# A transformer backbone on one core: the later modulation weights and the position-bias broadcasts go from SyncE's DMA queue to GpSimd's

## The chip, the cores and the metric

The kernel runs on one NeuronCore of a Trainium2 chip. The metric is the device time of one execution in microseconds (us). Engines are named as in the profile: PE (TensorE, matmuls), DVE (VectorE), ACT (ScalarE), POOL (GpSimd) and SP (SyncE, which here only issues DMAs). Each engine executes its instructions in the order of its own program.

## The reference

Two layers over 2048 latent tokens and 256 context tokens, of width 1024, in float32. Cut to what matters here:

```python
def _modulation(cvec, w_mod, b_mod):            # w_mod: (2 layers, 1024, 3072)
    return jnp.split(jax.nn.silu(cvec) @ w_mod + b_mod, 3, axis=-1)   # shift, scale, gate
```

Each layer normalises its tokens, scales and shifts them by the modulation (one vector for the latent tokens, from c, and one for the context tokens, from c_ctx), projects them to q, k, v and gate columns, runs two attention mixers, and adds the gated output projection to the residual. In layer 0 one of the mixers ("B") is a two-dimensional neighbourhood attention with a learned bias table b_rpb by relative position, 8 heads of 15 x 31 entries.

## The kernel before, in words

Work is cut into 9 pairs of token tiles (256 tokens each, the ninth being ctx). A tile scheduler sets the order of the instructions on every engine from a model of their times; the program's text gives the dependencies and a few constraints, so a changed line can move instructions on engines that the line does not name.

The first 330 us of layer 0, by `layer_front` (L939 and on), go like this.

- **Modulation, `mod_cols` (L144).** The 3072 columns of each layer are cut into 12 groups of 256; `j` counts them. Each group loads a 1 MB tile `wmod` (L148), from a pool of 4 buffers. For the first 8 groups of layer 0 (shift and scale, needed at once) and three groups of layer 1, PE multiplies `wmod` directly. For the other 13 groups DVE does the product: for the latent and, mostly, the context vector, 8 instructions on 128 x 256 elements accumulate into `macc` (the first on L159, seven on L161), 22 such sums or 176 instructions in all; then PE adds over partitions (pO<-macc), DVE copies the row (`m`, L171), PE transposes it and DVE adds the bias (`mod`, L177). The four remaining groups of layer 0 and the 12 of layer 1 form the filler `mods`, stepped in the program's text inside the loop over pairs of the second and third chunk (L1006 to L1008), behind the load of ctx (`xload[8]`) on the loading engine's queue and behind `shlast` on DVE's. `mod_scales` (L180) turns the first 8 groups into scales and shifts; its norm `hrs` is a POOL instruction.
- **hT, `hT_make` (L251).** For each pair, x is loaded, scaled by DVE (`xt`, L248), transposed by PE, scaled and shifted (`hf`, on DVE L272 and on ACT L270), cast to float16 (on DVE L274 and on ACT L276), and POOL subtracts to get the low half (L277), four times for a pair, 36 in all.
- **Projections, `project` (L306).** In chunks of 256 columns: qb0, kb0, vb0, and so on; 48 matmuls `pmm<-wk,hT` for a pair. qb0 runs beside the making of hT. q and k results are split into high and low halves `HL` (ACT L361, DVE L367), transposed by a DMA on SP's queue (L333) into `qkst` and stored (L335). v results go through `vst` (ACT L415, DVE L417).
- **Bias table, `rel_tables` (L598).** b_rpb and a reversed copy are each loaded into a tile `rp` of 120 x 128; then each of its rows is written 64 times into a DRAM scratch table `rpad`, by 4 DMAs for each table (L609), each of 1920 rows of 512 bytes. The B heads read them back in a skewed form (`braw`, L584), from 290 us on. In the text they stand at the third pair of the third chunk, held behind `self.wload`, the last weight load, on the loading engine's queue (L1003).

All these DMAs are issued by SP, in its order.

Of the kernel before, what the change touches and what calls it, by code (L numbers as in the profile page):

```python
# [16 lines left out]
P = 128  # L17
# [18 lines left out]
class Build:  # L36
# [107 lines left out]
    def mod_cols(self, l, j, wp, on_pe):  # L144

        nc = self.nc
        wt = wp.tile([P, 8, 256], F32, name="wmod")
        self.wlast = nc.sync.dma_start(out=wt, in_=self.I["w_mod"][l, :, j * 256:(j + 1) * 256].rearrange("(k p) j -> p k j", p=P))  # L148
        na = 1 if l == 1 and j >= 8 else 2
        terms = []  # L150
        if on_pe:
            terms = [(self.cT[:, :, k], wt[:, k]) for k in range(8)]
        else:
            for a in range(na):
                o = wp.tile([P, 256], F32, name="macc", bufs=4)
                for k in range(8):
                    c = self.cT[:, a, k:k + 1]
                    if k == 0:
                        nc.vector.tensor_scalar(out=o, in0=wt[:, k], scalar1=c, scalar2=None, op0=ALU.mult)  # L159
                    else:  # L160
                        nc.vector.scalar_tensor_tensor(out=o, in0=wt[:, k], scalar=c, in1=o, op0=ALU.mult, op1=ALU.add)  # L161
                    if k == 3:
                        yield
                yield
                terms.append((self.sel[:, 2 * a:2 * a + 2], o))
        pool = (self.pmm, "pmm") if l == 0 and j < 8 else (self.pO, "pO")
        ps = pool[0].tile([P, 512], F32, name=pool[1])
        for i, (l_, r_) in enumerate(terms):
            self.mm(ps[0:2, 0:256], l_, r_, i == 0, i == len(terms) - 1)
        m2 = wp.tile([2, 256], F32, name="m2", bufs=2)  # L170
        nc.vector.tensor_copy(out=m2, in_=ps[0:2, 0:256])  # L171
        pool = (self.ptr, "ptr") if l == 0 and j < 8 else (self.pO, "pO")
        ps2 = pool[0].tile([P, 512], F32, name=pool[1])
        for g in range(2):
            nc.tensor.transpose(out=ps2[:, 2 * g:2 * g + 2], in_=m2[:, g * P:(g + 1) * P], identity=self.idf[:2, :2])
        bias = self.bT[:, 24 * l + 2 * j:24 * l + 2 * j + 2].unsqueeze(2).broadcast_to([P, 2, 2])
        nc.vector.tensor_tensor(out=self.mod[l][:, 2 * j:2 * j + 2, :], in0=ps2[:, 0:4].rearrange("p (g a) -> p g a", a=2),  # L177
                                in1=bias, op=ALU.add)
# [419 lines left out]
    def rel_tables(self, pool):  # L598


        nc = self.nc
        self.rpad = []
        for t, name in enumerate(("b_rpb", "b_rpb_r")):
            rp = pool.tile([120, P], F32, name=f"rp{t}")
            nc.vector.memset(rp, 0.0)
            nc.sync.dma_start(out=rp[:, 48:79], in_=self.I[name].rearrange("o h r c -> (o h r) c"))
            rpad = self.dp.tile([120, 64, P], F32, name=f"rpad{t}")
            for i in range(0, 120, 30):
                nc.sync.dma_start(out=rpad[i:i + 30], in_=rp[i:i + 30].unsqueeze(1).broadcast_to([30, 64, P]))  # L609
            self.rpad.append(rpad)  # L610

    def b_tables(self):
# [969 lines left out]
```

## Time and profile before

| | |
|---|---|
| median of 3 runs | 3745.75 us (3744.8 to 3751.46) |
| the profiled execution | 3762.25 us |
| its span, first to last instruction | 3760.4 us |
| mean granted clock of PE | 0.983 |
| busy: PE, DVE, ACT, POOL | 3565.1, 2603.6, 2403.2, 2347.4 us |

The span is the profile's own time; 1.85 us of the profiled execution lie around it. Busy time is the time in which an engine executes, without the issuing of DMAs. The granted clock is the share of TensorE's full clock that the chip allowed.

### The profile page before, as it was taken

What the parts mean: (1) busy time and instruction counts of PE and PEld (TensorE: products, weight loads), DVE (VectorE), ACT (ScalarE), POOL (GpSimd) and SP (SyncE); (2) the same over time, 40 slices, a digit from 0 to 9 for tenths busy, and PEclk for the clock granted to TensorE, in tenths of its full rate; (3) what the DMA queues carried; (4) which work ended last, traced back from release to release, by engine and by line L of the source; (5) the groups of instructions that cost most, each with busy time, mean ns of one, the idle gap of its engine ahead of it and who ended that gap; (6) DMA issues with size and microseconds to landing.
All of it is one profiled execution on the core that took longest, in us unless ns stands there. A gap on an engine that the chain in (4) does not pass through costs nothing. (4 is left out here: it accounts for less than half of the span.)

```text
span 3760.4 us, 103033 instructions
## 1 busy us (share of the span) xinstructions
PE 3565.1 (95%) x42242; PEld 2946.7 (78%) x42242; DVE 2603.6 (69%) x6585; ACT 2403.2 (64%) x4094; POOL 2347.4 (62%) x1822
## 2 busy tenths in 40 slices
PE   7869998989999999999999999999989999999998
PEld 5648987878976777677767888999878888887775
DVE  5746779798567676666666888777565656656666
ACT  5215655556668887787864556666567777776665
POOL 3203456676358888788864454435358878877775
PEclk9989999999999999999999999999999999999999
DMA  7884634343261111111135444412351211211222
GB/s 235 214 210 103 124 88 101 80 92 101 67 213 40 44 60 38 48 49 49 33 114 135 104 101 100 105 58 78 113 168 30 78 47 56 62 37 51 101 98 103
DMA packets 455488, 350.64 MB, mean 93 GB/s; under 512 B 207782, under 2 KB 407270, under 8 KB 454502
## 3 DMA queue, kind: packets, MB, share of 16 engines
q1 hardware_dynamic: 455014, 344.06, 33.1%
q8 instruction: 330, 5.41, 0.6%
q14 instruction: 144, 1.18, 0.1%
HBM read 207.43 MB, written 106.90 MB: 84 GB/s over the span
## 5 line engine op out<-in xcount | busy, mean ns | idle before, releaser
L783 POOL TENSOR_TENSOR L<-Pm,H 128x1024 f16<-128x1024 f32 (+1 forms) x640 | 1240.1, 1958 | 293.0 <-ACT H L781 213.1
L82 PE MATMUL pmm<-wk,hT 128*128 128x256 f16 x10848 | 1365.5, 276 | 45.4 <-DVE HL L367 19.3
L82 PEld LDWEIGHTS <-hT 128*128 128x128 f16 x10848 | 1034.9, 99 | 189.6 <-issue 35.9
L752 DVE TENSOR_REDUCE mx<-pM 128x1 f32<-128x512 f32 (+1 forms) x1280 | 787.1, 634 | 514.0 <-PE pM L82 503.8
L82 PE MATMUL pO<-V,H 128*128 128x65 f16 (+3 forms) x9216 | 785.0, 207 | 3.2 <-DVE ya L1260 1.4
L82 PEld LDWEIGHTS <-H 128*128 128x128 f16 x9216 | 644.7, 98 | 100.5 <-DVE o L1454 3.6
L82 PE MATMUL pO<-V,L 128*128 128x65 f16 (+1 forms) x4608 | 710.8, 209 | 8.0 <-POOL L L783 7.4
L514 POOL TENSOR_TENSOR Pl<-Sb,Ph 128x640 f16<-128x640 f32 (+4 forms) x288 | 439.0, 1524 | 427.5 <-ACT Ph L513 248.3
L781 ACT CAST H<-Pm 128x1024 f16<-128x1024 f32 (+1 forms) x640 | 602.9, 959 | 11.8 <-PE pO L82 1.9
L82 PE MATMUL pS<-Qt,KH 128*128 128x256 f16 x2304 | 559.1, 273 | 2.6 <-DMA KH<-qk 1.4
L82 PE MATMUL pS<-Q,KL 65*128 65x256 f16 x2304 | 550.0, 274 | 0.0
L82 PEld LDWEIGHTS <-L 128*128 128x128 f16 x4608 | 442.9, 98 | 53.1 <-POOL L L783 14.9
L82 PE MATMUL pM<-KH,Qt 128*128 128x512 f16 (+1 forms) x1280 | 448.3, 359 | 16.4 <-DVE mx L752 10.3
L778 ACT ACTIVATE Pm<-pS,esc_c 128x1024 f32<-128x1024 f32 (+1 forms) x320 | 323.3, 1026 | 207.9 <-PE pS L82 181.7
L82 PEld LDWEIGHTS <-KL 65*128 65x128 f16 x3824 | 374.4, 98 | 83.3 <-issue 28.2
L778 ACT ACTIVATE Pm<-pS,esc_a 128x1024 f32<-128x1024 f32 (+1 forms) x320 | 324.6, 1027 | 156.1 <-PE pS L82 104.0
L82 PE MATMUL pX<-wo,yT 128*128 128x512 f16 x1488 | 390.2, 380 | 1.5 <-ACT yT L890 1.3
L82 PEld LDWEIGHTS <-KH 128*128 128x128 f16 x2304 | 227.3, 99 | 59.2 <-issue 7.0
L82 PEld LDWEIGHTS <-yT 128*128 128x128 f16 x1632 | 154.2, 98 | 134.4 <-ACT yT L890 6.2
L513 ACT CAST Ph<-Sb 128x640 f16<-128x640 f32 (+4 forms) x288 | 219.4, 762 | 51.1 <-PE pO L82 41.0
L82 PE MATMUL pT<-Q,K 128*128 128x128 f16 x1520 | 216.5, 220 | 18.1 <-ACT Sb L509 6.4
L82 PE MATMUL pT<-Q,KL 65*128 65x128 f16 x1520 | 214.5, 220 | 4.4 <-DVE Q L490 4.4
(295 smaller groups left out, 5536.5 us busy)
## 6 DMA issues: line engine op xcount, KB each, us to landing
qk<-qkst SPq DMA_DIRECT2D x104, 256.0 KB, 2.4
wmod<-w_mod SPq DMA_DIRECT2D x24, 1024.0 KB, 8.4
xo<-x SPq DMA_DIRECT2D x48, 512.0 KB, 3.5
xt<-x SPq DMA_DIRECT2D x34, 512.0 KB, 4.9
G<-zz SPq DMA_DIRECT2D x68, 256.0 KB, 2.5
x<-xo SPq DMA_DIRECT2D x34, 512.0 KB, 2.9
wst<-w_in_even SPq DMA_DIRECT2D x13, 1024.0 KB, 5.8
wst<-w_in_odd SPq DMA_DIRECT2D x13, 1024.0 KB, 5.5
```

Of the source, the lines that this page charges most:

```text
L82: return self.nc.tensor.matmul(out=out, lhsT=l, rhs=r, start=s, stop=e, skip_group_check=skip)
L513: nc.scalar.copy(out=H[:, :n * P], in_=Sb[:, :n * P])
L514: nc.gpsimd.tensor_tensor(out=L[:, :n * P], in0=Sb[:, :n * P], in1=H[:, :n * P], op=ALU.subtract)
L752: nc.vector.tensor_reduce(out=mx[:, j:j + 1], in_=ps[:, :n], op=ALU.max, axis=AX.X)
L778: nc.scalar.activation(out=Pm[:, :n], in_=S[:, :n], func=AF.Exp, scale=esc[0], bias=LNP)
L781: nc.scalar.copy(out=H[:, :n], in_=Pm[:, :n])
L783: eng.tensor_tensor(out=L[:, :n], in0=Pm[:, :n], in1=H[:, :n], op=ALU.subtract)
```

## The change

DMAs of wmod are issued by SP only for the first 8 groups of layer 0; the other 16 are issued by POOL. The 8 broadcasts into rpad are issued by POOL as well. What is computed does not change.

```diff
-        self.wlast = nc.sync.dma_start(out=wt, in_=self.I["w_mod"][l, :, j * 256:(j + 1) * 256].rearrange("(k p) j -> p k j", p=P))
+        q = nc.sync if l == 0 and j < 8 else nc.gpsimd
+        self.wlast = q.dma_start(out=wt, in_=self.I["w_mod"][l, :, j * 256:(j + 1) * 256].rearrange("(k p) j -> p k j", p=P))
...
             for i in range(0, 120, 30):
-                nc.sync.dma_start(out=rpad[i:i + 30], in_=rp[i:i + 30].unsqueeze(1).broadcast_to([30, 64, P]))
+                nc.gpsimd.dma_start(out=rpad[i:i + 30], in_=rp[i:i + 30].unsqueeze(1).broadcast_to([30, 64, P]))
```

The changed file has one line more from L149 on, so its L160 and L162 are L159 and L161 of before, and so on.

The order on SP, at the place of the rpad broadcasts, before:

```order
L606 DMA rp_2467<-b_rpb_r 120x31
L148 DMA wmod<-w_mod 128x8x256
L609 DMA rpad_2462<-rp_2459 1920x1x128 x2
L335 DMA qk_90<-qkst 128x4x256
L333 DMA_TRANSPOSE qkst<-HL 128x4x128 x2
L609 DMA rpad_2462<-rp_2459 1920x1x128 x2
L148 DMA wmod<-w_mod 128x8x256
L609 DMA rpad_2470<-rp_2467 1920x1x128 x4
L333 DMA_TRANSPOSE qkst<-HL 128x4x128
L335 DMA qk_90<-qkst 128x4x256
```

The same place on SP, now:

```order
L607 DMA rp_2467<-b_rpb_r 120x31
L336 DMA qk_90<-qkst 128x4x256
L334 DMA_TRANSPOSE qkst<-HL 128x4x128 x2
L336 DMA qk_90<-qkst 128x4x256
L334 DMA_TRANSPOSE qkst<-HL 128x4x128 x4
L336 DMA qk_90<-qkst 128x4x256 x2
```

Between the transposes and stores of q and k on SP there is no broadcast and no wmod load any more.

On POOL, the first rows behind the start of the program, now; before there was no DMA among them (`hT_449` and `hT_504` are the first two pairs, `xrs` and `wrs` norms of x and of a weight chunk):

```order
L121 TENSOR_TENSOR wrs<-n_309,mhalf 128x1
L149 DMA wmod<-w_mod 128x8x256 x4
L121 TENSOR_TENSOR xrs<-xr,mhalf 128x2
L121 TENSOR_TENSOR hrs<-n_428,mhalf 128x1
L278 TENSOR_TENSOR hT_449<-hf_455,hT_449 128x2x256
...
L278 TENSOR_TENSOR hT_504<-hf_510,hT_504 128x2x256
L149 DMA wmod<-w_mod 128x8x256
L278 TENSOR_TENSOR hT_504<-hf_529,hT_504 128x2x256
L149 DMA wmod<-w_mod 128x8x256
...
L149 DMA wmod<-w_mod 128x8x256
L121 TENSOR_TENSOR wrs<-n_1582,mhalf 128x1
L610 DMA rpad_2462<-rp_2459 1920x1x128 x4
L610 DMA rpad_2470<-rp_2467 1920x1x128 x4
L149 DMA wmod<-w_mod 128x8x256
L121 TENSOR_TENSOR wrs<-n_2384,mhalf 128x1
```

Of the 16 wmod loads 14 now stand ahead of the last hT subtraction, the fifteenth behind it, and the last behind the eight rpad broadcasts.

On DVE, where the first macc stand. Before they come beside the last two pairs (`hf_1219`, `hf_1315`; 20 of the 176 stand ahead of the last cast of hT):

```order
L272 TENSOR_SCALAR hf_1219<-pS,sc_82,sh_84 128x256 x2
L248 TENSOR_SCALAR xt<-xt,xrs 128x1024 x2
L159 TENSOR_SCALAR macc<-wmod,cT 128x256 x2
L161 SCALAR_TENSOR_TENSOR macc<-wmod,cT,macc 128x256 x3
L272 TENSOR_SCALAR hf_1238<-pT,sc_82,sh_84 128x256 x2
```

Now they begin ahead of the first pair (`hf_455`) and go on between all of them:

```order
L197 TENSOR_SCALAR sh_84<-mod_80,hrs 128x8x2
L160 TENSOR_SCALAR macc<-wmod,cT 128x256 x2
L442 TENSOR_SCALAR esc_b_3014<-F_0qb_305,hn_86 128x1
L273 TENSOR_SCALAR hf_455<-pS,sc_82,sh_84 128x256 x2
L162 SCALAR_TENSOR_TENSOR macc<-wmod,cT,macc 128x256 x5
L273 TENSOR_SCALAR hf_474<-pT,sc_82,sh_84 128x256 x2
L162 SCALAR_TENSOR_TENSOR macc<-wmod,cT,macc 128x256 x3
L160 TENSOR_SCALAR macc<-wmod,cT 128x256 x2
...
L418 SCALAR_TENSOR_TENSOR vst_1_169<-pmm,vst_1_169 128x4x64 x2
L160 TENSOR_SCALAR macc<-wmod,cT 128x256
L418 SCALAR_TENSOR_TENSOR vst_0_168<-pmm,vst_0_168 128x4x64 x2
```

128 of the 176 macc now stand ahead of the last cast of hT, 32 more beside kb0, and 16 in vb0; the first of those that need the last wmod (the row behind `vst_1_169`) stands ahead of the third pair's vst.

## Rows read from the trace of the kernel before

**Rows 1.** The page, part 1: busy us, share of the span, instructions.

```profile
PE 3565.1 (95%) x42242; PEld 2946.7 (78%) x42242; DVE 2603.6 (69%) x6585; ACT 2403.2 (64%) x4094; POOL 2347.4 (62%) x1822
```

**Rows 2.** Windows: stretch, length, engines' busy us (instructions), clock, DMA share, GB/s.

```profile
47.00:131.00 84.00, 68.62 (x546) 56.66 (x547) 70.27 (x127) 50.36 (x102) 53.15 (x47) 0.93 0.70 195
131.00:170.00 39.00, 38.49 (x328) 30.64 (x326) 29.39 (x80) 9.36 (x29) 1.52 (x2) 1.00 0.91 226
170.00:230.00 60.00, 30.07 (x171) 17.83 (x172) 22.62 (x62) 1.79 (x3) 0.00 (x0) 0.77 0.93 221
```

**Rows 3.** Timeline of PE, 160 to 285: start, us, operation, count, idle before.

```profile
174.62 0.28 PE L175 MATMUL pO<-idf,m 2*128 2x2 f32 x2 [5.13 <-DVE m L171]
174.84 4.79 PE L82 MATMUL pmm<-wk,hT 128*128 128x256 f16 x27
...
188.00 0.28 PE L175 MATMUL pO<-idf,m 2*128 2x2 f32 x2 [0.51 <-DVE m L171]
...
214.77 7.57 PE L82 MATMUL pmm<-wk,hT 128*128 128x256 f16 x48 [19.01 <-DVE HL L367]
225.35 0.59 PE L82 MATMUL pO<-macc,sel 128*2 128x256 f32 x2 [3.01 <-DVE macc L161]
226.45 1.01 PE L82 MATMUL pO<-macc,sel 128*2 128x256 f32 x2 [0.50 <-DVE macc L161]
227.40 6.42 PE L82 MATMUL pmm<-wk,hT 128*128 128x256 f16 x48
...
233.96 5.41 PE L82 MATMUL pmm<-wk,hT 128*128 128x256 f16 x48
...
268.14 1.01 PE L82 MATMUL pO<-macc,sel 128*2 128x256 f32 x2 [4.24 <-DVE mod L177]
269.08 5.76 PE L82 MATMUL pmm<-wk,hT 128*128 128x256 f16 x30
```

**Rows 4.** Timeline of ACT, 160 to 225.

```profile
213.40 0.60 ACT L361 ACTIVATE HL<-pmm 128x512 f16<-128x512 f32 x1 [39.87 <-DMA qkst<-HL]
```

**Rows 5.** Timeline of SP, 100 to 290: start of issue, us of issue.

```profile
101.02 0.43 SPq L148 DMA_DIRECT2D wmod<-w_mod  x1
...
182.34 18.79 SPq L609 DMA_DIRECT2D rpad<-rp  x4
201.22 8.49 SPq L333 DMA_TRANSPOSE qkst<-HL  x1
```

**Rows 6.** Windows of macc alone: PE, PEld and DVE busy us (instructions).

```profile
47.00:131.00 84.00, 0.00 (x0) 0.00 (x0) 16.36 (x26) 0.93 0.70 195
131.00:170.00 39.00, 4.10 (x16) 1.02 (x16) 22.46 (x56) 1.00 0.91 226
```

**Rows 7.** Timelines of POOL (first row) and DVE, 105 to 131.

```profile
124.19 2.70 POOL L277 TENSOR_TENSOR hT<-hf,hT 128x512 f16<-128x512 f32 x2 [3.11 <-ACT hT L276]
...
124.51 2.66 DVE L161 SCALAR_TENSOR_TENSOR macc<-wmod,cT,macc 128x256 f32<-128x256 f32 x2
127.10 0.41 DVE L274 CAST hT<-hf 128x512 f16<-128x512 f32 x1
...
129.72 1.66 DVE L161 SCALAR_TENSOR_TENSOR macc<-wmod,cT,macc 128x256 f32<-128x256 f32 x4
```

**Rows 8.** Groups by line, 47 to 131, POOL and DVE: busy us, mean ns, idle before.

```profile
L277 POOL TENSOR_TENSOR hT<-hf,hT 128x512 f16<-128x512 f32 x36 | 45.8, 1286 | 28.0 <-DVE hT L274 18.5 <-ACT hT L276 9.5
...
L274 DVE CAST hT<-hf 128x512 f16<-128x512 f32 x18 | 10.8, 612 | 3.4 <-ACT hf L270 3.4
```

**Rows 9.** Tiles wmod and rpad: issue ns min/median/max, first and last us; wmod's landing.

```profile
L148 SPq DMA_DIRECT2D wmod<-w_mod x24: 379/700/6928, 2.7 to 257.1; - x24
...
DMA to landing us min/median/max: 5.4/8.4/12.9
...
L609 SPq DMA_DIRECT2D rpad<-rp x8: 902/2978/7840, 156.2 to 195.8; - x8
```

**Rows 10.** Timeline of DVE, 255 to 290.

```profile
265.29 0.35 DVE L159 TENSOR_SCALAR macc<-wmod,cT 128x256 f32<-128x256 f32 x1 [6.69 <-DMA wmod<-w_mod]
```

## Prediction

> **What bounds the kernel now.** I read the page first: TensorE (PE) is busy for 3565.1 of 3760.4 us [rows 1], so only a stretch in which PE is short of work can give much back. The change alters the order of the engines in the first 330 us or so, so next I took the busy time of every engine in that part by stages [rows 2]. The reader is to see three things there. From 47 to 131 us, where the transposed activations (hT) are made, PE has 68.6 of 84 us and VectorE (DVE) 70.3. From 131 to 170 PE is full. From 170 to 230 PE has 30.1 of 60 us at a mean granted clock of 0.77 of full speed, and DMA engines are 93% busy.
>
> The timeline of PE names the holes of that last stage [rows 3]: 5.13 us before 174.62, 19.01 before 214.77, 3.01 before 225.35 and 4.24 before 268.14, all put down to DVE. With six waits of 0.26 to 1.01 us from 188.00 to 226.45, 3.3 us together, the holes sum to 34.7 us. The longest is not DVE's own: DVE waits for ScalarE (ACT), which sat idle for 39.87 us until the DMA that reads HL (the split q and k) freed its buffer [rows 4]. That DMA is a transpose on SP's queue, and SP was issuing rpad broadcasts: four took 18.79 us to issue, and the transpose behind them another 8.49 [rows 5]. So the stall is SP's queue, held up by the table of position biases. After each hole PE runs slow for a while: 48 matmuls took 7.57 and 6.42 us where they take 5.41 later, 27 took 4.79 where 27/48 of 5.41 is 3.04, and 30 took 5.76 where it is 3.38 [rows 3]. That is 2.2 + 1.0 + 1.7 + 2.4 = 7.3 us more. All that this stall can give back is 34.7 + 7.3 = **42 us**, 1.1% of the time.
>
> **The change part by part.** *What it removes.* SP loses 16 wmod loads and 8 rpad broadcasts; the transposes of HL stand behind no rpad any more. I count the whole 42 us as gained, less some 4 us for waits on modulation sums that stay in this stage (48 of the 176 accumulations still stand behind the hT work): four like the 1.01 and 0.5 us waits of now. The other end is that the transposes still share the DMA engines with rpad and half of the stall stays; that is a rival below.
>
> *What it moves on DVE, the term that decides.* The wmod loads stood behind the load of ctx on SP, and so began at 101.02 us [rows 5]. On GpSimd's (POOL) queue nothing holds them there, and the order on DVE follows: 128 of the 176 accumulations (macc) now stand ahead of the last cast of the hT work, where 20 stood before, so 108 more. DVE executes in order, so each of them delays every hT step behind it. Their price: from 131 to 170 us 56 of them keep DVE busy for 22.46 us, 0.401 each; inside the hT stage 26 took 16.36, 0.629 each [rows 6]. The difference shows in the timeline: in the 2.70 us in which POOL did two hT subtractions, DVE finished two macc in 2.66 us, while four take 1.66 us once POOL is done [rows 7]. Instructions of DVE that read SBUF alone wait until the running subtraction of POOL ends. So 108 cost 43.3 us at the one price and 67.9 at the other. POOL has 36 subtractions [rows 8]; DVE's casts of hT, 612 ns in the mean, already pay the same toll at some of them (one that ran while POOL was idle took 0.41 [rows 7]), so the toll on macc cannot grow with their number. I take a third of the difference: 43.3 + 8 = 51 us. Against it stand the 13.7 us that DVE was idle in this stage [rows 2]. Half of these idle us come from waits on ACT and POOL that move along with the work, so I let 7 be filled. **The hT stage grows by 51 - 7 = 44 us**; its ends are 43.3 - 13.7 = 29.6 and 67.9. PE can't fill this time: its projections need hT pair by pair and stand behind it in PE's order, and PE was idle for only 15.4 us there.
>
> The Trainium skill bears on this in "SBUF — State Buffer", section "SBUF: two separate sides": a two-port operation of VectorE keeps GpSimd out of the port pair that they share, and a DMA issued from GpSimd then can't have its descriptors written, so that the transfer waits. [...]
>
> *What it adds on POOL.* 14 of the wmod issues now stand among POOL's work of the hT stage, 4 of them ahead of the first modulation norm (hrs). POOL has no DMA issue in the trace, so I bound one by SP's: 0.38 to 6.93 us, median 0.70, for wmod [rows 9]. At 0.70 the 14 make 10 us, and POOL has 84 - 53.2 = 30.9 us idle in the stage [rows 2]: nothing on the path. I take this value, since most of SP's long ones stand where its queue was full of rpad. At 6.93 they make 97 us and POOL would set the end; this is a rival. An issue on POOL also waits for its buffer (four of them), which DVE's macc free, but these stand in the same order on DVE.
>
> *What is late next.* The last wmod load stands on POOL behind all eight rpad broadcasts, and its macc stand on DVE ahead of the v splits (vst) of the third and later pairs of vb0. In the trace of before rpad was issued from 156.2 us on [rows 9], and ACT went on, behind the transpose that followed the last of it, at 213.40 [rows 4]: 57 us for all eight, beside other transfers. If POOL issues them at about 131 + 44 + 13 = 188 (two pairs of projections behind the longer stage), they are through some 55 us later, at 243, and the last wmod 8 us after that [rows 9], at 251. The third pair of vb0 is projected about 11.5 pairs of 5.41 us after the stage's end, plus 12 us of modulation products, at 175 + 62 + 12 = 249. So the wait lies between 0 and some 20 us (if rpad starts or runs 20 us later; in before DVE waited 6.69 us for the last wmod [rows 10]); I take 8.
>
> *The sum.* +44 (hT stage) - 42 (stall) + 4 (waits that stay) + 8 (last wmod) = **+14 us**. From about 305 us on the order of every engine but for one row is what it was, so this carries to the end. Against the profiled execution, 3762.25 us, that is 3776; the runs shown have a median of 3745.75, 16.5 lower, and the forecast is made against that: **3760 us**. The ends of the terms give 29.6 - 42 = -12 and 67.9 - 42 + 4 + 20 = +50.
>
> **The rivals.**
>
> *The longer hT stage is cheap, and the stall's end is kept: faster.* Place: DVE from 47 to 131 us. If macc fill all of DVE's 13.7 idle us, pay no toll and the last wmod is in time, the sum is -12: 3734 us. The point from which it decides is a growth of the hT stage of 22 us with the other terms as forecast, or 34 us with those at nothing. For it speaks that PE was busy for 68.6 of the 84 us although macc and hT work already mix in the last 20 of them; against it that only 20 macc did this, and 108 more are to.
>
> *The toll is on POOL: slower by far.* If an issue on POOL takes what SP's longest took, POOL has 53.2 + 97 = 150 us of work in a stage that I put at 128, 22 us more, and the 8 rpad issues (2.98 us each in the median [rows 9]) stand ahead of POOL's next weight norm, which PE needs: some 10 us. 3760 + 32 = 3792 us. Against it: nothing in the trace shows a POOL issue. [...]
>
> *The queue of their own does not separate them: slower.* rpad's packets keep the DMA engines 93% busy wherever they are issued [rows 2], and the transposes and the qk stores go through the same engines. If half of the stall stays, 21 us are not gained: 3760 + 21 = 3781. For it: the DMA share of 0.91 to 0.93 in these stages. Against it: SP's issue was held up in order behind rpad (18.79 us for four), which can't recur. The Trainium skill, "DMA: Bandwidth & Descriptors", section "Issuing engines are not separate DMA queues", says that transfers of all issuing engines run on the same 16 DMA engines and that issuing from several saves only the time of the sequencer. The share in the rows agrees with the first half; the 18.79 us of issue speak against the "usually small" that it gives the second. By it alone the sum would be the 3781 of this rival.
>
> **How the numbers follow.** A measurement of this kernel can tell 0.2%, 7.5 us, from no change. The forecast has a chance of 0.52, with a range of its own of 3748 to 3776; 0.08 of it lies within 7.5 us of no change. The faster rival has 0.24, of which 0.18 is faster by over 7.5 us. The POOL rival has 0.13, all slower. The shared engines have 0.11, of which 0.03 would come out near no change, since the growth may be at its low end. So faster 0.18, same 0.08 + 0.06 + 0.03 = 0.17, slower 0.65. The range, 3730 to 3796, takes in the faster rival's time and the POOL rival's, and leaves out the ends at which all terms go one way.
>
> **What would show it.** Right: macc starting at about 50 us; the last hT subtraction on POOL at 165 to 185 us instead of 128; DVE above 9 of 10 us from 55 us on; no ACT HL waiting over 10 us for qkst; PE's hole of 19 us gone; DVE waiting for the last wmod in vb0. Wrong: the last subtraction before 155 us (then faster); POOL's sequence with holes of 5 us and more at the wmod rows (POOL rival); ACT still waiting for qkst by tens of us (shared engines). A change in the order's later part, beyond 330 us, would make the whole argument wrong.

## The result, and the profile after

| | before | after |
|---|---|---|
| median of 4 runs | 3748.61 us | 3788.78 us (3787.54 to 3794.67) |
| ratio, 95% interval | | 1.0109 [1.009, 1.0128] |
| the profiled execution | 3762.25 us | 3788.29 us |
| its span | 3760.4 us | 3786.5 us |

The change makes the kernel slower by 40 us. The profiled executions differ by 26 only: that of before lies 14 us above its median, that of after at it.

The page of after has the queue that the change opens, q0, beside SP's q1:

```profile
PE 3564.7 (94%) x42242; PEld 2945.8 (78%) x42242; DVE 2608.6 (69%) x6585; ACT 2401.9 (63%) x4094; POOL 2378.9 (63%) x1846
...
q1 hardware_dynamic: 422894, 319.41, 30.4%
q0 software_dynamic: 6528, 24.65, 2.5%
```

PE does the same work in 26 us more of span (3565.1 before [rows 1]); over the whole span, what was lost was lost waiting. POOL is busy for 31.5 us more (2378.9 against 2347.4): its 24 DMA issues now count as busy time, 23.5 us, and its hT subtractions take some 9 us longer.

The windows of after, first from 47 us to the end of the longer hT stage (181) and then to the first scores of the B heads (337), with a window of macc alone behind them:

```profile
47.00:181.00 134.00, 93.28 (x616) 65.65 (x617) 122.10 (x256) 54.69 (x116) 73.31 (x57) 0.83 0.64 186
181.00:337.00 156.00, 116.31 (x964) 94.26 (x963) 45.80 (x126) 27.44 (x83) 17.47 (x29) 0.86 0.74 149
...
47.00:181.00 134.00, 9.04 (x28) 1.71 (x28) 68.93 (x129) 0.83 0.64 186
```

These answer to [rows 2] and [rows 6]. Before, the first scores began at 301.02 us, and the stretch from the end of hT to them reads:

```profile
129.00:301.00 172.00, 137.06 (x1043) 100.95 (x1042) 90.42 (x252) 27.47 (x83) 8.00 (x19) 0.90 0.78 195
```

So the first part is 52 us longer (134 against 82) and the second 16 shorter (156 against 172), +36 us at the first scores. In the second part PE is busy for 20.8 us less and idle for 39.7 instead of 34.9: the stall has not gone. Most of the 20.8 us is work that moved into the first part, by windows of the modulation products (tile pO) alone, behind the end of hT, before and after:

```profile
128.90:301.02 172.12, 27.93 (x124) 9.58 (x124) 9.02 (x32) 0.00 (x0) 0.90 0.78 194
180.90:337.31 156.41, 11.98 (x48) 4.05 (x48) 4.51 (x16) 0.00 (x0) 0.86 0.74 150
```

76 of the 124 products, 16.0 us, are done in the hT stage now. The projections did not move: 914 matmuls `pmm` stand behind hT before and 913 after, but they take 106.3 us in place of 112.4.

From the start to the first scores, before and after, the same matmuls run:

```profile
0.00:301.02 301.02, 238.33 (x1740) 170.83 (x1741) 174.25 (x440) 93.33 (x231) 63.99 (x78) 0.92 0.78 212
0.00:337.31 337.31, 245.17 (x1741) 174.56 (x1741) 180.92 (x440) 93.77 (x231) 97.35 (x102) 0.86 0.73 189
```

Of the 36.3 us more, 29.4 are idle time of PE, and 6.8 are the same matmuls at a lower granted clock (0.86 in the mean, before 0.92). Behind the first scores the profiled execution of before is 10 us the longer one: its remaining 40504 matmuls keep PE busy for 3326.8 us, those of after for 3319.5. So the profiled executions end only 26 us apart.

PE's timeline of after has it in two holes instead of [rows 3]:

```profile
226.01 6.72 PE L82 MATMUL pmm<-wk,hT 128*128 128x256 f16 x48 [9.84 <-DVE HL L368]
260.88 8.03 PE L82 MATMUL pmm<-wk,hT 128*128 128x256 f16 x48 [28.15 <-DVE HL L368]
```

Behind them stands the same wait of ACT as in [rows 4], SP's transposes as in [rows 5], and now the rpad issues on POOL, by their timelines:

```profile
259.51 0.60 ACT L362 ACTIVATE HL<-pmm 128x512 f16<-128x512 f32 x1 [34.28 <-DMA qkst<-HL]
...
225.09 31.87 SPq L334 DMA_TRANSPOSE qkst<-HL  x4
...
208.22 7.60 POOL L610 DMA_DIRECT2D rpad<-rp  x7 [16.14 <-DMA rp<-b_rpb]
```

POOL issues seven broadcasts in 7.6 us, and SP then needs 31.87 us for four transposes, although no broadcast stands in its own queue. The DMA view of 208 to 262 us shows what moves meanwhile: packets, MB and share of the 16 engines for each queue, then the median us from issue to landing of SP's stores and transposes. The last row is the view of both from 205 to 262.

```profile
q0 software_dynamic: 2176, 7.87, 78.0%
q1 hardware_dynamic: 5217, 1.76, 27.8%
...
qk<-qkst SPq DMA_DIRECT2D x3, 256.0 KB, 2.3
qkst<-HL SPq DMA_TRANSPOSE x7, 6.7
...
DMA to landing us min/median/max: 2.3/2.9/33.7
```

The packets of POOL's queue take 78% of the 16 engines' time over 54 us, 42 us for 7.87 MB; with the 27.8% of SP's that is more than the whole, so packets of the two overlap. A packet of POOL's queue holds 3.6 KB, one of SP's 0.34 KB. From the first broadcast's issue until ACT goes on, 51 us pass (208.22 to 259.51), where 57 did before [rows 4, rows 9]. Not everything that shares the engines waits: the qk stores landed after 2.3 us in the median, the latest transfer after 33.7.

The longer hT stage is plain in more rows of the timelines of after: DVE's first hf; six macc on DVE, and beside them one subtraction on POOL that takes 3.13 us (the shortest takes 1.14); the longest macc, and the subtractions beside it; and the last of the subtractions:

```profile
52.29 0.99 DVE L273 TENSOR_SCALAR hf<-pS,sc,sh 128x256 f32<-128x256 f32 x2
...
90.58 2.44 DVE L162 SCALAR_TENSOR_TENSOR macc<-wmod,cT,macc 128x256 f32<-128x256 f32 x6
...
91.38 3.13 POOL L278 TENSOR_TENSOR hT<-hf,hT 128x512 f16<-128x512 f32 x1 [8.00 <-ACT hT L277]
...
97.74 4.23 DVE L160 TENSOR_SCALAR macc<-wmod,cT 128x256 f32<-128x256 f32 x1
...
98.43 3.38 POOL L278 TENSOR_TENSOR hT<-hf,hT 128x512 f16<-128x512 f32 x3
...
178.65 2.27 POOL L278 TENSOR_TENSOR hT<-hf,hT 128x512 f16<-128x512 f32 x2 [0.36 <-DVE hT L275]
```

### The profile page after: what moved, and what is told of

Read it like the earlier page. It is cut to its first block, busy times and chain, and to the rows that moved or that the text cites. A ratio compares the mean times of both kernels' runs of the same rounds, so it can differ in the third digit from the quotient of the medians.

```text
span 3786.5 us, 103051 instructions
## 1 busy us (share of the span) xinstructions
PE 3564.7 (94%) x42242; PEld 2945.8 (78%) x42242; DVE 2608.6 (69%) x6585; ACT 2401.9 (63%) x4094; POOL 2378.9 (63%) x1846
## 5 line engine op out<-in xcount | busy, mean ns | idle before, releaser
L82 PE MATMUL pT<-Q,K 128*128 128x128 f16 x1520 | 218.2, 221 | 17.5 <-DVE Sb L506 10.6
```

The lines of the kernel that those rows point to most:

```text
L82: return self.nc.tensor.matmul(out=out, lhsT=l, rhs=r, start=s, stop=e, skip_group_check=skip)
```

## The experiments

The theory after the result: two causes that have nothing to do with each other. (1) The macc stand ahead of the hT work on DVE because their loads left SP's order; the hT stage is longer by what they take. (2) The stall in kb0 comes from rpad's volume on the DMA engines, which all queues share; the queue that issues it does not matter. Rivals: the stall is SP's order (then moving rpad must help by itself), or POOL's queue is slow as such.

**e1: rpad alone on POOL.**

```diff
-        q = nc.sync if l == 0 and j < 8 else nc.gpsimd
+        q = nc.sync
```

> Only the rpad broadcasts on POOL, every wmod load on SP. Theory: the stall in kb0 comes from rpad's packets on the DMA engines that the HL transposes share, whichever engine issues them, and the rest of the loss from the macc that moved ahead of the hT work. So here the last hT subtraction ends at about 129 us as before, and PE's holes in kb0 (before 34.7 us, changed kernel 39.7) stay at 25 to 45 us: 3735 to 3765 us in all. Rival: the stall is the order of SP's queue; then the holes go and the time is 3705 to 3720 us.

Measured: 3755.32 us against 3752.6, ratio 1.0003 [0.9993, 1.0012]. The timeline of PE:

```profile
178.01 0.37 PE L176 MATMUL pO<-idf,m 2*128 2x2 f32 x2 [9.17 <-DVE m L172]
211.29 7.36 PE L82 MATMUL pmm<-wk,hT 128*128 128x256 f16 x48 [18.53 <-DVE HL L368]
```

The last subtraction ends at 128.1 us, and two holes, together 27.7 us, remain. Moving rpad to POOL's queue is worth nothing, and SP's order alone is not what stalls. Not excluded is that POOL's queue holds SP's transfers back in a way of its own: from 130 to 300 us the transposes and qk stores landed up to 46.4 us after their issue here, 10.6 before. No run put rpad on a third queue.

**e2: the wmod loads alone on POOL.**

```diff
-                nc.gpsimd.dma_start(out=rpad[i:i + 30], in_=rp[i:i + 30].unsqueeze(1).broadcast_to([30, 64, P]))
+                nc.sync.dma_start(out=rpad[i:i + 30], in_=rp[i:i + 30].unsqueeze(1).broadcast_to([30, 64, P]))
```

> Only the later wmod loads on POOL, the rpad broadcasts on SP. Theory: 128 macc stand ahead of the last hT cast, so the last hT subtraction ends at 175 to 185 us, the rpad stall stays, and the time is that of the changed kernel, 3775 to 3795 us. Rival: the loss comes from rpad being issued by POOL, and the longer hT stage is made up later; then about 3750 us.

Measured: 3781.27 us, ratio 1.0073 [1.0054, 1.0091]; the hT stage ends at 178.8 us, as expected. The larger part of the loss belongs to the wmod loads. The sum of e1 and e2, 2.7 + 28.7 us, falls some 9 short of the 40. In the traces e2's first scores come at 327.66 us, 9.7 ahead of those of the changed kernel: 2 of it at the end of hT, and PE is idle behind it for 33.5 us instead of 39.7. So rpad on POOL costs some us when the wmod loads are there as well, though nothing alone; why is open.

**e2h: as e2, with macc held on DVE behind the casts of the eighth pair.**

```diff
+                self.hcast[p] = nc.vector.tensor_copy(out=hT[:, 2 * kk:2 * kk + 2, 0], in_=tf)
...
-                    with self.tc.issue_after(self.xload[self.xpn].ins), self.tc.issue_after(shlast):
+                    with self.tc.issue_after(self.xload[self.xpn].ins), self.tc.issue_after(self.hcast[7].ins):
```

> As e2 (later wmod loads on POOL, rpad on SP), and the modulation sums are held on DVE behind the casts of hT of the eighth pair, so that 23 macc stand ahead of the last hT cast instead of 128. Theory: the longer hT stage came from the order on DVE alone; the last hT subtraction ends at 128 to 135 us again, the rpad stall on SP stays, 3745 to 3765 us, no different from before. Rival: wmod loads on POOL's queue cost by themselves (their issue, or DVE and POOL at one port); then the last hT subtraction ends after 145 us and the time is over 3770.

Measured: 3762.91 us, ratio 1.0025 [1.0014, 1.0035]. With the loads still on POOL, holding macc takes 20 of e2's 28.7 us away (8.7 are left), and the hT stage ends at 143.5 us instead of 178.8. It holds most of the loads back too, for they wait for buffers that macc free: four are issued by 143.5 us, in e2 eleven. The stage's expected end (128 to 135) and "no different from before" are misses: the first hf starts at 52.28 us as after the change (46.67 before), so the stage starts late, and ends 15 us late.

**e9: as e2h, with the loads held on POOL behind subtractions of the seventh pair.**

```diff
+            self.hsub[p] = nc.gpsimd.tensor_tensor(out=hT[:, 2 * kk:2 * kk + 2, 1], in0=tf, in1=hT[:, 2 * kk:2 * kk + 2, 0],
...
-                    with self.tc.issue_after(self.xload[self.xpn].ins), self.tc.issue_after(self.hcast[7].ins):
+                    with self.tc.issue_after(self.xload[self.xpn].ins), self.tc.issue_after(self.hcast[7].ins), self.tc.issue_after(self.hsub[6].ins):
```

> As e2h, and on POOL the later wmod loads are held behind hT subtractions of the seventh pair, so that none is issued while x is still loaded at 30 to 50 us. Theory: what e2h still lost (hT's first step at 52 us instead of 47 and the last subtraction at 143.5 instead of 128.9) came from wmod loads competing with the loads of x; here the first hf starts at 47 us, the last hT subtraction ends at 128 to 134, and the time is 3745 to 3757 us, within 0.2% of before. Rival: the loads on POOL's queue cost by themselves; then the hT stage stays at 140 us or more and the time at 3760 or more.

Measured: 3765.34 us, ratio 1.0034 [1.0023, 1.0044]. Timelines of DVE, POOL and PE:

```profile
46.68 0.99 DVE L275 TENSOR_SCALAR hf<-pS,sc,sh 128x256 f32<-128x256 f32 x2
...
132.65 1.15 POOL L280 TENSOR_TENSOR hT<-hf,hT 128x512 f16<-128x512 f32 x1 [0.36 <-DVE hT L277]
...
229.10 7.20 PE L82 MATMUL pmm<-wk,hT 128*128 128x256 f16 x48 [25.05 <-DVE HL L370]
```

The stage is as expected: it starts at 46.68 us, so the early wmod loads did delay its start by 5.6 us, and it ends at 133.8. The time is a miss: 13 us above before instead of none. The holes behind rpad, still on SP here, are 25.05 and 8.85 us, and the first scores start at 307.75, 6.7 us later than before. That accounts for half of the 13 us; the rest stays open, as does whether loads on POOL cost something by themselves once neither order nor start is disturbed.

**e4: the change, with rpad held on POOL behind a later norm.**

```diff
+        self.plast = self.nc.gpsimd.tensor_tensor(out=out, in0=in_, in1=self.mhalf[:, :w], op=ALU.pow)
...
+        self.wpow = self.plast
...
-                    with self.tc.issue_after(self.wload.ins):
+                    with self.tc.issue_after(self.wload.ins), self.tc.issue_after(self.wpow.ins):
                         self.rel_tables(sp)
```

> The changed kernel with the rpad broadcasts held on POOL behind the norm of the weight chunk that follows vb0 (wrs of qb1), that is behind nearly all HL transposes of kb0. Theory: the two holes of 9.8 and 28.2 us that PE had behind HL go, the hT stage stays 52 us longer: about 3745 us, 3735 to 3762. Rival: the transposes are slow for another reason (the wmod traffic, SP's own order): then within 10 us of 3788. A third: rpad comes too late for the first B head and its braw loads, and up to 20 us of the gain are lost again.

Measured: 3788.61 us, ratio 1.0091 [1.0072, 1.011], beside 1.0109 for the change: no gain beyond the noise. The time is within 10 us of 3788, as the first rival has it, but not by its cause: from the end of hT to 296 us PE has no hole of 0.7 us or more, so the transposes of kb0 no longer stall. The stall moved with rpad into vb0, where the v stores wait. The waits of e4 (us in total, times, longest) and its PE timeline:

```profile
ACT vst L417 <- DMA v<-vst: 60.6, 2, 49.9
...
296.34 0.37 PE L176 MATMUL pO<-idf,m 2*128 2x2 f32 x2 [38.78 <-DVE m L172]
```

The theory is right that rpad makes the holes of kb0, and its hope that vb0 has room for rpad is wrong.

**e5: wmod on SP, rpad on POOL and held as in e4.** The two edits of e1 and e4 together.

> wmod loads all on SP as before, rpad on POOL and held behind the same norm of qb1's weights. Theory: neither cost is left: hT ends at about 129 us, no hole over 10 us in kb0, 3705 to 3725 us, faster than both kernels. Rival: if the stall is only moved into vb0 (the v stores or the first braw wait for rpad), 3735 to 3750 us.

Measured: 3750.76 us, ratio 0.9993 [0.9983, 1.0002]: the rival, 0.8 us above its range. One hole again, by PE's timeline:

```profile
251.99 1.68 PE L82 MATMUL pmm<-wk,hT 128*128 128x256 f16 x7 [32.69 <-DVE vst L419]
```

In e1, e4 and e5 rpad is issued from 156, 240 and 201 us on, and the kernel stalls each time, behind transposes in e1 and behind v stores in e4 and e5.

**e7: the kernel before, with rpad in pieces of 2 KB.**

```diff
-            rp = pool.tile([120, P], F32, name=f"rp{t}")
+            rp = pool.tile([120, 4, P], F32, name=f"rp{t}")
...
+            nc.gpsimd.tensor_copy(out=rp[:, 1:4], in_=rp[:, 0:1].broadcast_to([120, 3, P]))
...
+            self.nc.sync.dma_start(out=self.rpad[t][i].rearrange("r (a k) p -> r a (k p)", k=4),
+                                   in_=src.unsqueeze(1).broadcast_to([30, 64 // 4, 4 * P]))
```

> The kernel before, all DMAs on SP, with each row of the table laid out four times in SBUF first, so that the broadcast moves pieces of 2 KB instead of 512 bytes; the bytes are the same. Theory: the cost of rpad is by piece; its time on the DMA engines falls to half or less, PE's holes in kb0 to 10 to 20 us: 3725 to 3742 us. Rival: the cost is by byte (writes to DRAM); then nothing changes, 3745 to 3757.

Measured: 3754.88 us, ratio 0.9999 [0.999, 1.0008]. From 155 to 215 us a broadcast landed 15.3 us after its issue in the median, before 13.6. Pieces of 2 KB in place of 512 bytes change nothing: the time is the rival's, and the cost does not go by the piece between these sizes.

**e6: the kernel before, with rpad cut by heads.** Only the two parts that heads 0 and 1 read stay where they were, the other six go into the three chunks behind vb0; all on SP.

```diff
-            for i in range(0, 120, 30):
-                nc.sync.dma_start(out=rpad[i:i + 30], in_=rp[i:i + 30].unsqueeze(1).broadcast_to([30, 64, P]))
+            self.rpad.append([self.dp.tile([30, 64, P], F32, name=f"rpad{t}_{i}") for i in range(4)])
+        self.rel_piece(0)
...
+                if l == 0 and p == 3 and ci in (3, 4, 5):
+                    with self.tc.issue_after(self.wload.ins):
+                        self.rel_piece(ci - 2)
```

> The kernel before, all DMAs on SP, with the broadcast in four parts for each table, of which the two parts for heads 0 and 1 stay where they were and the other six are issued one pair of them in each of the three chunks that follow vb0. Theory: what stalls is the volume of rpad on the shared DMA engines at one time; a quarter of it is left in kb0, PE's holes there fall from 34.7 to under 15 us and the later parts fall where the DMA engines are half idle: 3715 to 3735 us. Rival: the later parts stall the stores and loads there as long: 3745 to 3755.

Measured: 3734.53 us, ratio 0.9943 [0.9927, 0.996], at the expected range's upper end. One hole above 3 us is left behind hT, at a place where ACT waits up to 14.6 us for v stores and two parts of rpad stand between them on SP:

```profile
239.96 0.37 PE L175 MATMUL pO<-idf,m 2*128 2x2 f32 x2 [7.35 <-DVE m L171]
```

**e10: as e6, the later parts one chunk later each.**

```diff
-                if l == 0 and p == 3 and ci in (3, 4, 5):
+                if l == 0 and p == 3 and ci in (4, 5, 6):
...
-                        self.rel_piece(ci - 2)
+                        self.rel_piece(ci - 3)
```

> As e6, with the six later parts of rpad one chunk later each, so that none falls beside the v stores of vb0. Theory: e6's last hole of 7.35 us in vb0 (v stores behind two parts of rpad) goes: 3722 to 3732 us. Rival: the parts stall another store further on, or the first two parts make up what is left: 3733 to 3740.

Measured: **3724.2 us, ratio 0.9925 [0.991, 0.9939]** to before, 65 us under the changed kernel. The windows and PE's largest hole between 131 and 283 us:

```profile
131.00:190.00 59.00, 55.50 (x434) 41.53 (x432) 39.13 (x106) 11.15 (x32) 1.46 (x1) 0.94 1.03 237
190.00:240.00 50.00, 50.00 (x398) 36.53 (x396) 36.98 (x106) 10.71 (x31) 0.85 (x2) 1.00 0.88 236
...
182.56 0.37 PE L175 MATMUL pO<-idf,m 2*128 2x2 f32 x2 [2.78 <-DVE m L171]
```

PE is busy for all 50 us from 190 to 240, where before it had 30.1 of the 60 us from 170 to 230 [rows 2], and the first scores come at 264.15 us instead of 301.02. This is the version to keep: every DMA on SP, and a table loaded when it is needed. It shows the second theory from its other side, since it changes neither the queue nor the bytes, only how many of them move at one time. It changes SP's order too; that this order alone is not the cause rests on e1.

## Why the prediction was right, and where it was wrong

The direction held, and the time lies in the range (3730 to 3796), but 29 us above the forecast of 3760 and outside the forecast's own 3748 to 3776. The longer hT stage was foreseen; the stall that was to pay for it stayed.

- **The hT stage, forecast +44 us: right.** First hf to the end of the last subtraction took 82.2 us before (46.67 to 128.9) and 128.6 after (52.29 to 180.9), +46.4. By its parts, between these ends: macc 127 in 68.2 us in place of 22 in 14.8, 53.4 more where 51 were forecast; of the 13.7 idle us of DVE 4.4 were filled (9.4 are left), where I gave 7; DVE's other work took 2.7 us less. e2h confirms the cause: macc were held behind the casts there, and the stage ended 35 us earlier than in e2.
- **The toll on macc: near in size, one-sided in mechanism.** At 0.401 the 129 macc from 47 to 181 us would take 51.7 us and took 68.9, a toll of 17 us; 6 were there before, so 11 came where I let 8 come. I had DVE wait for the running subtraction of POOL. The rows of after show one macc of 4.23 us beside a run of three, and the opposite as well: six macc at full pace beside one subtraction of 3.13 us. The toll sits in few of them: the median of L162's hardly moved (471 ns; 467 before, from 131 to 170 us). POOL's subtractions took 1.54 us in the mean instead of 1.29.
- **The start of the stage: not foreseen.** The first hf came 5.6 us later, because the first four wmod loads are issued from 31 to 43 us now, beside the loads of x. I had asked what the loads wait for and not whom they delay. e9, which holds them back, has its first hf at 46.68 again.
- **The stall, forecast -42 + 4 us: the step that failed.** "So the stall is SP's queue, held up by the table of position biases" took the place where the wait showed for its cause. PE's idle time behind hT is 39.7 us after, 34.9 before. SP's issue is slow without rpad in its order too: after the change its four transposes still take 31.87 us to issue. e1, with rpad alone moved, shows no gain; e6 and e10, with rpad spread out, show the gain. The rival of the shared engines was the right one, and I gave it 0.11 and half of the stall; it was the whole, and its 3781 should have been 3798 (3760 + 42 - 4). The Trainium skill's sentence on it ("DMA: Bandwidth & Descriptors", "Issuing engines are not separate DMA queues"), which I let the 18.79 us of issue speak against, agrees with these traces.
- **The last wmod behind rpad, forecast +8 us: nothing.** No macc behind 181 us waited for a DMA. POOL issued the last load at 276.25 us, and what held it was not rpad but a buffer that a macc freed.
- **Work that PE did earlier: left out.** In the longer stage PE also did 76 modulation products that had stood behind it, and the stretch behind hT has 20.8 us less of PE work, 16.0 of it these products. I had written that PE can't fill the time; for the projections that held, but the products follow the macc, and these I had moved ahead.
- **The issues on POOL, forecast nothing: right.** The 16 loads took 0.88 to 1.15 us of POOL each, 0.92 in the median; the 8 rpad issues 1.06 to 1.19. The Trainium skill's rule ("SBUF — State Buffer", "SBUF: two separate sides") by which a DMA issued from GpSimd waits for its descriptors beside a two-port operation of VectorE does not show here: the loads landed 7.7 us after their issue in the median, on SP before 8.4. Whether macc are such operations no run shows.

From the rows of the two profiles: +5.6 (start) + 46.4 (stage) + 4.8 (more idle behind it) - 20.8 (less PE work behind it) = +36.0 us, against +36.3 read at the first scores; the profiled executions end 26 us apart and the medians 40.2. The two large errors of the forecast, 43 us on the stall (-38 for +4.8) and 21 on the PE work, went opposite ways. That the range held the time is in part luck: with the 16.0 us of modulation products left behind the stage the time would have been near 3805, outside it.

## What to carry to other kernels

A wait that names a queue's DMA has two possible causes, the order of the queue and the time of the engines behind it. Neither the wait nor the DMA share tells them apart: the share was 0.93 in the stalled stretch of before [rows 2] and 1.03 in e10 from 131 to 190 us, where PE was busy for 55.5 of 59. Moving the suspect alone to another queue shows whether that queue helps (e1). Where it does not, move fewer bytes at one time, or move them when they are needed (e6, e10). And a load that loses its place in one queue can take its consumers' order with it, here 108 more macc in front of the hT work; look at what now stands in front of the work that the next engine waits for.

## What the runs showed that was not expected

- Transfers of POOL's queue go in packets of 3.6 KB for the same 512-byte rows of rpad (7.87 MB in 2176 packets). SP's transfers beside them landed up to 33.7 us after their issue in kb0, and the v stores of e5 up to 20.6 us.
- An issue on POOL took 0.88 to 1.19 us, all 24 of them, while SP's issues of wmod took between 0.38 and 6.93 us [rows 9]. POOL's queue can still hold POOL up: the eighth broadcast was issued 4.4 us late, waiting for an earlier one.
- DVE and POOL can cost each other more than one instruction's wait when both work on SBUF: macc went from 0.401 to 0.534 us in the mean, one of them to 4.23, and one subtraction of POOL to 5.38.
